# Sums of weight blocks made by accumulating DMA in DRAM instead of on VectorE and GpSimd, and SiLU as a sigmoid with two products

## The chip, the cores and the metric

The kernel runs on one core of a Trainium2 chip. The metric is the time of one execution on the device, in microseconds (us). A core has TensorE (PE in the profile; its weight loads, which overlap its matmuls, are PEld), VectorE (DVE), ScalarE (ACT), GpSimd (POOL) and the queue of SyncE (SP), from which this kernel issues nearly all of its DMAs.

## The reference, cut to what matters

One layer of a streaming encoder: 1024 frames of 1024 features, a token mixer with two branches (HGRN heads and banded attention), a gated feed-forward part, and a gated per-layer input.

```python
h = rmsnorm(x, norm_mix_g[li])
z = h @ w_in[li]
...
merged = (jax.nn.sigmoid(gate_a) * (oa @ w_branch_a[li])
          + jax.nn.sigmoid(gate_b) * (ob @ w_branch_b[li]))
x = x + merged @ w_out[li]
h2 = rmsnorm(x, norm_ffn_g[li])
x = x + (jax.nn.silu(h2 @ w_ffn_gate[li]) * (h2 @ w_ffn_up[li])) @ w_ffn_down[li]
h3 = rmsnorm(x, norm_ple_g[li])
x = x + jax.nn.sigmoid(h3 @ w_ple_gate[li]) * (p[li].astype(x.dtype) @ w_ple_proj[li])
```

`D_FF` is 2816, that is 22 blocks of 128. The change is in how `merged @ w_out`, the feed-forward part's `@ w_ffn_down` and its `silu` are computed.

## The kernel before, in words

Every large product is made from float32 operands that are split in two parts, a rounded high part (`wh`, `whi`: a cast on ACT) and the rest (`wl`, `wlo`: a subtraction, mostly on POOL); TensorE makes three products of these parts. Weights stream from DRAM into raw tiles `wr`, 512 KB each.

The layer runs in stages, one behind the other on TensorE: norm and HGRN heads; attention (from about 290 us to 490); the mixer's gates (500 to 650); branches and output projection (to 820); the feed-forward gate and up projections (820 to 1292); the down projection (1292 to 1550); the per-layer input (to the end).

From the mixer's gates on, the large products use Strassen's scheme in Winograd's form: seven block products in place of eight, of sums of blocks. Of the weights of the output projection (4 groups of four blocks, called quads) and of the down projection (11 quads) the sums are S1 = A21 + A22, S3 = A11 − A21, S2 = S1 − A11 and S4 = A12 − S2. They are made ahead of time and stored in DRAM (`spill`), from where `passes` loads them as weights when the projection comes. A block of a quad is 128 x 512. Sums of the activations (T1 to T4) are made on VectorE, by `branch_sums` for the output projection and by `keep_acts` for the down projection; each product is added into its target by the function that `added` returns.

Who made the weights' sums before: the first five quads (`QUADS = 5`: all four of the output projection and one of the down projection) on POOL in `gate_units`, by `quad_slow`, four POOL additions of 128x512 each; the other ten on VectorE in the feed-forward stage, by `quad_pieces`: two halves per quad, each loaded into one tile named `qd` (its pool has one buffer), four VectorE additions of 128x256, four stores of 128 KB.

The feed-forward stage runs in units, `ff_pairs` looping over units 1 to 21 (unit 0 stands before it). Even units make two blocks of the gate projection, odd ones the same blocks of the up projection. A unit is one call of `strassen`: seven products of 12 matmuls of 512 columns, and VectorE additions of the products in `t` tiles (`u2`, `u3` in the code) and with the row of norm factors `rb`. Between products `strassen` calls `next(side)`: `side` prepares the next unit's weights (`strassen_weights`: block sums `q` on VectorE, casts on ACT, `wlo` on POOL and one on VectorE), the activation sums (`keep_acts`), and pieces of the quads. After each half block, `unit_gate` multiplies by `rb` on VectorE, applies SiLU on ACT and multiplies by `rb` on POOL (the tile `s<-t,rb` on POOL in the profile); `unit_up` multiplies gate and up together.

What sets the order: each engine works strictly in the order in which the program names its instructions (`order` ties each instruction to the one before it on its engine, and so the SP queue too). An instruction that waits holds up all that stand behind it on that engine. Nothing is rescheduled; a `yield` in a generator is the place at which another stream's next step is put. Waits come from data and from tiles whose buffers come free: the feed-forward pools hold 7 `tmp` tiles (`t`) and one `quad` tile (`FFN`).

Most of the profile's lines are the helper's line 54, through which all pinned instructions go; so tiles, not lines, tell them apart.

Of the kernel before, what the change touches and what calls it, by code (L numbers as in the profile page):

```python
# [31 lines left out]
RAW = 2  # L32
AHEAD = 3
PLAIN = 4
QUADS = 5


C_MIX, C_FFN, C_PLE, C_ON, C_GQ, C_GK, C_LB = 0, 8, 16, 24, 25, 26, 27
# [18 lines left out]
class Trunk:  # L57
# [580 lines left out]
    def attention(self):  # L638
# [33 lines left out]
        for i in range(FIRST, 8):  # L672
            next(feed, None)
            if i == FIRST:
                self.hgrn_gate()
            if i == 7:
                drain(stack(0))
                drain(self.hgrn_out())
        for n in range(whole + 2):
            stage(n - 1, 1)  # L680
            next(feed, None)
            if n < whole:
                if steps[n][1] == 0:
# [24 lines left out]
            if n >= whole:  # L708
                next(tail)
            yield 0  # L710
# [83 lines left out]
        while self.kept:  # L794
            self.store(*self.kept.pop(0))

    def gate_units(self, sums):

        V, A = self.V, self.A
        h0, h1 = slice(0, HALF), slice(HALF, T)  # L800
# [39 lines left out]
        for n in range(units):  # L840

            def side():
                more = self.strassen_weights() if n + 1 < units else self.branch_first()
                if n == 0:
                    yield
                    yield
                next(more, None)
                if n + 2 < units:
                    self.strassen_load()
                yield  # L850
                for _ in more:
                    next(sums, None)
                    yield

            self.strassen(lambda c, half, ps: self.gate_done(PLAIN + 2 * n + c, half, ps), side(), early=n == 0)
            yield 0
# [93 lines left out]
    def branch_sums(self, i):  # L950

        m, V = self.m, self.V
        for kind in ("T2", "T1", "T4"):
            m[kind, i] = self.slot()
        V.tensor_tensor(m["B12", i], m["B22", i], m["B12", i], ALU.subtract)
        m["T3", i] = m["B12", i]
        V.tensor_tensor(m["T2", i], m["T3", i], m["B11", i], ALU.add)
        V.tensor_tensor(m["T1", i], m["B22", i], m["T2", i], ALU.subtract)
        V.tensor_tensor(m["T4", i], m["B21", i], m["T2", i], ALU.subtract)


# [49 lines left out]
    def added(self, x):  # L1011

        h0, h1 = slice(0, HALF), slice(HALF, T)
        to = {"A11": ((1, h0), (0, h1), (1, h1)), "S2": ((0, h1),), "A12": ((0, h0),), "S3": ((1, h1),),
              "S1": ((1, h1),), "A22": ((1, h0),), "S4": ((0, h1),)}

        def after(kind, u, ps):
            for odd, h in to[kind]:
                t = x(2 * u + odd)[:, h]
                self.V.tensor_tensor(t, ps, t, ALU.add)  # L1020

        return after

# [21 lines left out]
            if V is self.V:  # L1045
                yield

    def quad_slow(self, jobs):

        G = self.nc.gpsimd  # L1050

        def load(src):
            w = [self.slot() for _ in range(2)]
            for j in range(2):
                self.load(w[j], src[:, j * D:j * D + D])
            return [t[:, i * HALF:i * HALF + HALF] for t in w for i in range(2)]

        def store(parts, k, sums):
            for kind, part in zip(("S2", "S3", "S1", "S4"), parts):
                if k % 2 == 0:  # L1060
                    sums[kind, k // 2] = self.spill()
                self.store(sums[kind, k // 2][:, k % 2 * HALF:k % 2 * HALF + HALF], part)

        cur, prev = load(jobs[0][0]), None
        yield
        yield
        for n, (_, k, sums) in enumerate(jobs):
            a11, a21, a22, a12 = cur
            G.tensor_tensor(a22, a21, a22, ALU.add)
            if prev:  # L1070
                store(*prev)
            yield
            G.tensor_tensor(a21, a11, a21, ALU.subtract)
            yield
            G.tensor_tensor(a11, a22, a11, ALU.subtract)
            prev = cur, k, sums
            if n + 1 < len(jobs):
                cur = load(jobs[n + 1][0])
            yield
            G.tensor_tensor(a12, a12, a11, ALU.subtract)  # L1080
            yield
        store(*prev)

    def quad_pieces(self, jobs):

        V, cols = self.V, HALF // 2
        for src, k, sums in jobs:
            for half in range(2):
                self.n += 1
                w = self.fp.tile([P, 4 * cols], F32, tag="quad", name=f"qd{self.n}")  # L1090
                at = slice(half * cols, half * cols + cols)
                self.load(w[:, :].rearrange("p (i c) -> p i c", i=4), src.rearrange("p (i c) -> p i c", i=4)[:, :, at])
                yield
                yield
                a11, a21, a22, a12 = [w[:, i * cols:i * cols + cols] for i in range(4)]
                V.tensor_tensor(a22, a21, a22, ALU.add)
                V.tensor_tensor(a21, a11, a21, ALU.subtract)
                yield
                V.tensor_tensor(a11, a22, a11, ALU.subtract)
                V.tensor_tensor(a12, a12, a11, ALU.subtract)  # L1100
                yield
                for kind, part in zip(("S2", "S3", "S1", "S4"), (a11, a21, a22, a12)):
                    if k % 2 == 0 and half == 0:
                        sums[kind, k // 2] = self.spill()
                    self.store(sums[kind, k // 2][:, k % 2 * HALF + at.start:k % 2 * HALF + at.stop], part)
                yield

    def quad_plan(self, plain, npairs, sums):
        order = []
# [8 lines left out]


    def out_proj(self):  # L1120
        split, ready = self.m_split, self.m_ready

        def operand(b, i):
# [271 lines left out]
    def unit_gate(self, c, half, ps):  # L1395
# [2 lines left out]
        hs = slice(half * HALF, half * HALF + HALF)  # L1398
        s = self.stmp()
        V.tensor_tensor(g[:, hs], ps, self.rb[:, hs], ALU.mult)  # L1400
        A.activation(s, g[:, hs], AF.Silu)
        G.tensor_tensor(g[:, hs], s, self.rb[:, hs], ALU.mult)

    def unit_up(self, c, half, ps):
        hs = slice(half * HALF, half * HALF + HALF)
# [103 lines left out]
    def keep_acts(self, k):  # L1509
# [5 lines left out]
        def keep(kind, src):  # L1515
# [5 lines left out]
        keep("B21", b[:, h0])  # L1521
        keep("B22", b[:, h1])
        yield
        V.tensor_tensor(a[:, h1], b[:, h1], a[:, h1], ALU.subtract)
        yield
        yield
        V.tensor_tensor(a[:, h0], a[:, h1], a[:, h0], ALU.add)
# [10 lines left out]
    def ff_pairs(self):  # L1538
# [1 line left out]

        units = len(self.sorder)
        self.acts = {}
        pieces = self.quad_pieces(self.later)
        self.strassen_load()
        for n in range(1, units):
            if n % 2 == 0:
# [2 lines left out]
            def side():  # L1549
# [13 lines left out]
                if n % 4 == 0:  # L1563
                    next(pieces, None)
                if n == units - 2:
                    drain(pieces)

            self.strassen((self.unit_gate, self.unit_up)[n % 2], side())
            if n % 2 == 1:
# [3 lines left out]
    def down_plan(self):  # L1573

        n = NFF // 2
        self.aorder = [(b, i, min(D, n * HALF - i * D)) for _, b in self.KINDS for i in range(STEPS)]
        self.plan_weights(self.quad_plan(self.d["dw"], n, self.sums) + self.worder2)
        self.anext, self.araw, self.aready = 0, [], []

# [280 lines left out]
    def run(self):  # L1860
# [18 lines left out]
        with ExitStack() as es:  # L1879
# [24 lines left out]
            with ExitStack() as xs:  # L1904
                self.qp = Small(tc, xs, QUARTERS, "gate_", reuse_waits="tile")
                self.fp = Small(tc, xs, FFN, "gates_", reuse_waits="tile")
                jobs = [(d["oq"][k], k, self.osums) for k in range(4)] + [(d["wq"][k], k, self.sums) for k in range(NFF // 2)]
                drain(self.gate_units(self.quad_slow(jobs[:QUADS])))
                self.later = jobs[QUADS:]
# [158 lines left out]
```

## Time and profile before

| | us |
|---|---|
| median of 3 runs | 1604.16 |
| lowest, highest | 1602.46, 1605.62 |
| the profiled execution | 1605.46 |
| its span in the trace | 1603.7 |
| TensorE busy (share of the span) | 1558.6 (97%) |
| VectorE busy | 1163.0 (73%) |
| GpSimd busy | 652.3 (41%) |
| ScalarE busy | 638.2 (40%) |
| mean granted clock of TensorE | 0.993 |

A profile row of the timeline reads: start, duration, engine, line, operation, output tile <- input tiles, shapes, how many, and in brackets how long the engine had been idle before and what released it. Groups read: line, engine, operation, tiles, count, then busy time and mean duration in ns, then idle time before them and its cause. Buffer numbers are left out of the names: `t` is any temporary, `s` any of the large 128x1024 slots, `pm` a PSUM tile, `d` a spill in DRAM, `q` a block sum of the unit's weights, `in_...` an input of the kernel. "x2" merges two like instructions. The duration of an instruction in the trace holds whatever it waits for once it has been started.

### The profile page before, as it was taken

What the parts mean: (1) busy time and instruction counts of PE and PEld (TensorE: products, weight loads), DVE (VectorE), ACT (ScalarE), POOL (GpSimd) and SP (SyncE); (2) the same over time, 40 slices, a digit from 0 to 9 for tenths busy, and PEclk for the clock granted to TensorE, in tenths of its full rate; (3) what the DMA queues carried; (4) which work ended last, traced back from release to release, by engine and by line L of the source; (5) the groups of instructions that cost most, each with busy time, mean ns of one, the idle gap of its engine ahead of it and who ended that gap; (6) DMA issues with size and microseconds to landing.
All of it is one profiled execution on the core that took longest, in us unless ns stands there. A gap on an engine that the chain in (4) does not pass through costs nothing. (4 is left out here: it accounts for less than half of the span.)

```text
span 1603.7 us, 21710 instructions
## 1 busy us (share of the span) xinstructions
PE 1558.6 (97%) x8224; PEld 1313.0 (82%) x8224; DVE 1163.0 (73%) x1754; ACT 638.2 (40%) x1059; POOL 652.3 (41%) x341
## 2 busy tenths in 40 slices
PE   8999999999999999999999999999999999999997
PEld 6998998888888888888888777777777888888886
DVE  5656656378787787447898898888788867755677
ACT  5221221177676633312566222222222234445462
POOL 3422221313121087335313555544455544644553
PEclk9999999999999999999999999999999999999999
DMA  5101000210202575744445345444444379885334
GB/s 187 53 28 53 27 28 27 99 40 28 86 15 94 190 251 194 289 178 183 132 149 191 124 149 170 151 145 140 141 154 153 123 269 336 297 274 188 125 115 174
DMA packets 95337, 230.40 MB, mean 144 GB/s; under 512 B 9984, under 2 KB 31104, under 8 KB 94720
## 3 DMA queue, kind: packets, MB, share of 16 engines
q1 hardware_dynamic: 95088, 229.00, 41.1%
q8 instruction: 64, 1.05, 0.3%
q14 instruction: 41, 0.34, 0.1%
q10 hardware_dynamic: 144, 0.02, 0.0%
HBM read 163.70 MB, written 65.27 MB: 143 GB/s over the span
## 5 line engine op out<-in xcount | busy, mean ns | idle before, releaser
L83 PE MATMUL pm<-s,wh 128*128 128x512 f32 (+1 forms) x1712 | 531.0, 391 | 6.5 <-ACT wh L123 5.3
L83 PE MATMUL pm<-s,whi 128*128 128x512 f32 x1568 | 489.1, 393 | 20.1 <-DVE t L54 20.1
L126 POOL TENSOR_TENSOR wl<-wr,wh 128x1024 fp32r<-128x1024 f32 (+2 forms) x108 | 267.6, 2483 | 401.1 <-ACT wh L123 397.8
L83 PEld LDWEIGHTS pm<-s,wh 128*128 128x128 f32 x1712 | 319.1, 188 | 73.4 <-ACT wh L123 5.3
L83 PEld LDWEIGHTS pm<-s,whi 128*128 128x128 f32 x1568 | 296.0, 190 | 86.9 <-DVE t L54 25.6
L83 PE MATMUL pm<-s,wl 128*128 128x512 f32 (+1 forms) x856 | 333.3, 389 | 0.5 <-POOL wl L126 0.5
L54 DVE TENSOR_TENSOR s<-s,s 128x512 f32<-128x512 f32 (+4 forms) x217 | 263.5, 1244 | 82.3 <-ACT s L54 44.7
L83 PE MATMUL pm<-s,wlo 128*128 128x512 f32 x784 | 307.3, 392 | 0.0
L83 PE MATMUL pm<-wh,s 128*128 128x256 f32 (+1 forms) x896 | 237.6, 340 | 0.0
L123 ACT CAST wh<-wr 128x1024 fp32r<-128x1024 f32 (+2 forms) x114 | 115.0, 1010 | 270.5 <-PE pm L83 147.6
L83 PEld LDWEIGHTS pm<-s,wl 128*128 128x128 f32 x856 | 160.9, 188 | 34.4 <-POOL wl L126 1.2
L83 PEld LDWEIGHTS pm<-s,wlo 128*128 128x128 f32 x784 | 148.6, 190 | 31.9 <-DVE wlo L54 0.5
L83 PEld LDWEIGHTS pm<-wh,s 128*128 128x128 f32 x896 | 154.4, 190 | 14.0
L54 DVE TENSOR_TENSOR t<-pm,t 128x512 f32<-128x512 f32 x138 | 94.9, 688 | 89.9 <-PE pm L83 83.4
L54 POOL TENSOR_TENSOR wlo<-wr,whi 128x512 fp32r<-128x512 f32 (+1 forms) x53 | 116.2, 2200 | 95.0 <-ACT whi L54 95.0
L54 DVE TENSOR_TENSOR s<-pm,s 128x512 f32<-128x512 f32 (+1 forms) x134 | 87.1, 681 | 89.4 <-PE pm L83 89.2
L83 PE MATMUL pm<-wl,s 128*128 128x256 f32 (+1 forms) x448 | 147.5, 329 | 0.8 <-POOL wl L126 0.8
L54 POOL TENSOR_TENSOR s<-t,rb 128x512 f32<-128x512 f32 x44 | 70.3, 1601 | 115.4 <-ACT t L54 115.4
L54 POOL TENSOR_TENSOR wlo<-q,whi 128x512 fp32r<-128x512 f32 x52 | 83.5, 1606 | 79.5 <-ACT whi L54 73.2
L54 ACT CAST s<-s 128x1024 fp32r<-128x1024 f32 (+1 forms) x94 | 90.0, 980 | 60.7 <-DVE s L54 36.1
L54 ACT CAST whi<-q 128x512 fp32r<-128x512 f32 (+1 forms) x81 | 61.4, 758 | 120.3 <-PE pm L83 98.7
L54 ACT ACTIVATE t<-s 128x512 f32<-128x512 f32 x44 | 27.8, 633 | 167.2 <-DVE s L54 164.3
(145 smaller groups left out, 1856.0 us busy)
## 6 DMA issues: line engine op xcount, KB each, us to landing
s<-d SPq DMA_DIRECT2D x67, 512.0 KB, 5.6
d<-s SPq DMA_DIRECT2D x107, 256.0 KB, 2.6
wr<-d SPq DMA_DIRECT2D x36, 512.0 KB, 3.7
wr<-in_sg SPq DMA_DIRECT2D x22, 512.0 KB, 4.8
wr<-in_su SPq DMA_DIRECT2D x22, 512.0 KB, 4.9
s<-in_x SPq DMA_DIRECT2D x21, 512.0 KB, 7.5
qd<-in_wq SPq DMA_DIRECT2D x20, 512.0 KB, 3.7
d<-qd SPq DMA_DIRECT2D x80, 128.0 KB, 1.9
```

The costliest lines, as they stand in the source:

```text
L54: return lambda *a, **k: self.trunk.order(op(*a, **k), self.key)
L83: return self.order(self.nc.tensor.matmul(*a, **k))
L123: self.nc.scalar.copy(hi[:, c], raw[:, c])
L126: rest.tensor_tensor(lo[:, c], raw[:, c], f32(hi[:, c]), ALU.subtract)
```

## The change

The sums of weights are no longer made by an engine. In the attention loop, `dma_sums` issues one plain copy per step on SP, from the input's block in DRAM to the sum's spill in DRAM (32 copies: 8 of the output projection, 24 of the down projection, each of two quads' blocks, 512 KB). Later, 32 DMAs issued by POOL add a second operand onto the spill in transit (`accum_op=ALU.add`): 8 in `gate_units`, where the POOL additions stood, and 24 in the odd (up) units of `ff_pairs`, up to three per unit. Since such a DMA can only add, the lower blocks' part is taken with the other sign: S3 = A11 + A21, S2 = S1 + A11, S4 = A12 + S2. `added` then subtracts some products in place of adding them, and `branch_sums` and `keep_acts` swap operands. `quad_slow`, `quad_pieces`, the `qd` tile, their loads and stores go.

Two more things: the 128x1024 sum at the end of `keep_acts` is written as two of 128x512; and SiLU in `unit_gate` becomes a Sigmoid on ACT followed by two products on POOL in place of one. The `tmp` pool has 8 tiles in place of 7.

```diff
@@ the attention loop
+        self.osum = self.dma_sums(self.d["oq"], 4, self.osums)
+        self.wsum = self.dma_sums(self.d["wq"], NFF // 2, self.sums)
+        copies = chain(islice(self.osum, 8), islice(self.wsum, 4 * STEPS))
         for n in range(whole + 2):
+            next(copies, None)
             stage(n - 1, 1)
@@ gate_units, side()
-                for _ in more:
-                    next(sums, None)
+                for i, _ in enumerate(more):
+                    if i % 2:
+                        next(self.osum, None)
                     yield
@@ branch_sums
-        V.tensor_tensor(m["B12", i], m["B22", i], m["B12", i], ALU.subtract)
+        V.tensor_tensor(m["B12", i], m["B12", i], m["B22", i], ALU.subtract)
...
@@ added
+        plus, minus = ALU.add, ALU.subtract
+        to = {"A11": ((1, h0, minus), (0, h1, plus), (1, h1, minus)), "S2": ((0, h1, minus),), "A12": ((0, h0, plus),),
+              "S3": ((1, h1, plus),), "S1": ((1, h1, minus),), "A22": ((1, h0, plus),), "S4": ((0, h1, plus),)}
...
-                self.V.tensor_tensor(t, ps, t, ALU.add)
+                self.V.tensor_tensor(t, t, ps, op)
@@ new, in place of quad_slow and quad_pieces
+    def dma_sums(self, src, n, sums):
...
+        for i in jobs:
+            for kind, q in (("S1", 1), ("S3", 0), ("S2", 0), ("S4", 3)):
+                sums[kind, i] = self.spill()
+                self.load(cut(part(kind, i)), block(i, q))
                 yield
...
+        add = lambda out, x: self.G.dma_start(out, x, accum_op=ALU.add, max_dma_last_dim=4 * T)
+        for j in range(0, len(jobs), 2):
+            for kind in ("S1", "S3", "S2", "S4"):
+                for i in jobs[j:j + 2]:
+                    if kind in ("S1", "S3"):
+                        add(cut(part(kind, i)), block(i, 2 if kind == "S1" else 1))
+                    else:
+                        add(part(kind, i), part("S1" if kind == "S2" else "S2", i))
+                    yield
@@ unit_gate
-        A.activation(s, g[:, hs], AF.Silu)
-        G.tensor_tensor(g[:, hs], s, self.rb[:, hs], ALU.mult)
+        A.activation(s, g[:, hs], AF.Sigmoid)
+        G.tensor_tensor(g[:, hs], g[:, hs], s, ALU.mult)
+        G.tensor_tensor(g[:, hs], g[:, hs], self.rb[:, hs], ALU.mult)
@@ keep_acts
-        V.tensor_tensor(
-            b[:, :].rearrange("p (two t) -> p two t", two=2), b[:, :].rearrange("p (two t) -> p two t", two=2),
-            a[:, h0].unsqueeze(1).to_broadcast([P, 2, HALF]), ALU.subtract)
+        V.tensor_tensor(b[:, h0], b[:, h0], a[:, h0], ALU.subtract)
+        V.tensor_tensor(b[:, h1], a[:, h0], b[:, h1], ALU.subtract)
@@ ff_pairs, side()
-                for _ in more:
+                for i, _ in enumerate(more):
                     next(keep, None)
-                    if n > 1:
-                        next(pieces, None)
+                    if n % 2 and i % 2 == 0:
+                        next(self.wsum, None)
                     yield
...
-FFN = {"q1024": 1, "q512": 3, "raw": 2, "tmp": 7, "quad": 1}
+FFN = {"q1024": 1, "q512": 3, "raw": 2, "tmp": 8}
```

On POOL, a gate unit of the feed-forward stage (an `s` written from `t` and `rb` is the last step of `unit_gate`; `wlo` belongs to the next unit's weights) and what follows it in the up unit, before:

```order
L54 TENSOR_TENSOR s_9576<-t_9661,rb_8400 128x512
L54 TENSOR_TENSOR wlo_9642<-wr_9459,whi_9641 128x1024
L54 TENSOR_TENSOR s_9575<-t_9684,rb_8400 128x512
L54 TENSOR_TENSOR wlo_9666<-q_9622,whi_9665 128x512
L54 TENSOR_TENSOR s_9576<-t_9712,rb_8400 128x512
L54 TENSOR_TENSOR s_9575<-t_9737,rb_8400 128x512
L54 TENSOR_TENSOR wlo_9742<-q_9716,whi_9741 128x512
```

And after the change:

```order
L53 TENSOR_TENSOR s_9830<-s_9830,t_9916 128x512
L53 TENSOR_TENSOR s_9830<-s_9830,rb_8393 128x512
L53 TENSOR_TENSOR wlo_9899<-wr_9720,whi_9898 128x1024
L53 TENSOR_TENSOR s_9829<-s_9829,t_9938 128x512
L53 TENSOR_TENSOR s_9829<-s_9829,rb_8393 128x512
L53 TENSOR_TENSOR wlo_9922<-q_9879,whi_9921 128x512
L53 TENSOR_TENSOR s_9830<-s_9830,t_9960 128x512
L53 TENSOR_TENSOR s_9830<-s_9830,rb_8393 128x512
L53 TENSOR_TENSOR s_9829<-s_9829,t_9988 128x512
L53 TENSOR_TENSOR s_9829<-s_9829,rb_8393 128x512
L53 TENSOR_TENSOR wlo_9994<-q_9965,whi_9993 128x512
```

Each of the four half blocks now has two products in a row, and the `wlo` between them stand behind one or more products that were not there.

On POOL, an up unit after the change (before, the same `wlo` stood there without the DMAs; `d` is a spill):

```order
L53 TENSOR_TENSOR wlo_9715<-wr_9559,whi_9714 128x512
L53 DMA d_4377<-d_4216 128x1024
L53 TENSOR_TENSOR wlo_9756<-wr_9561,whi_9755 128x1024
L53 DMA d_4647<-d_4510 128x1024
L53 TENSOR_TENSOR wlo_9775<-q_9736,whi_9774 128x512
L53 DMA d_4436<-d_4377 128x1024
L53 TENSOR_TENSOR wlo_9826<-q_9808,whi_9825 128x512
```

Three DMAs have come in between the `wlo` of the next gate unit.

On VectorE, from the middle of a gate unit on, before (`qd` are the removed sums; `s` from `s` are the activation sums; `t` from `pm` are the additions of products):

```order
L54 TENSOR_TENSOR s_9575<-s_9576,s_9575 128x512
L54 TENSOR_TENSOR qd_9850<-qd_9850 128x256 x2
L54 TENSOR_TENSOR wlo_9940<-q_9906,whi_9939 128x1024
L54 TENSOR_TENSOR qd_9850<-qd_9850 128x256 x2
L54 TENSOR_TENSOR t_9975<-pm_9890,t_9904 128x512
L54 TENSOR_TENSOR t_9975<-pm_9891,t_9975 128x512
L54 TENSOR_TENSOR s_9888<-t_9975,rb_8400 128x512
L54 TENSOR_TENSOR s_9575<-s_9575 128x512
L54 TENSOR_TENSOR s_9887<-pm_9889,rb_8400 128x512
L54 TENSOR_TENSOR s_9576<-s_9576,s_9575 128x1024
```

And after:

```order
L53 TENSOR_TENSOR s_9533<-s_9533,s_9534 128x512
L53 TENSOR_TENSOR wlo_9882<-q_9848,whi_9881 128x1024
L53 TENSOR_TENSOR t_9913<-pm_9832,t_9846 128x512
L53 TENSOR_TENSOR t_9913<-pm_9833,t_9913 128x512
L53 TENSOR_TENSOR s_9830<-t_9913,rb_8393 128x512
L53 TENSOR_TENSOR s_9533<-s_9533 128x512
L53 TENSOR_TENSOR s_9829<-pm_9831,rb_8393 128x512
L53 TENSOR_TENSOR s_9534<-s_9534,s_9533 128x512
L53 TENSOR_TENSOR s_9534<-s_9533,s_9534 128x512
```

The two pairs of `qd` sums around `wlo` are gone, and the one sum of 128x1024 is two of 128x512.

More of the change, by code (lines that the diff above doesn't have):

```diff
@@ L34 @@
 PLAIN = 4
-QUADS = 5
 C_MIX, C_FFN, C_PLE, C_ON, C_GQ, C_GK, C_LB = 0, 8, 16, 24, 25, 26, 27
@@ L795, in gate_keep, with gate_units @@
             self.store(*self.kept.pop(0))
-    def gate_units(self, sums):
+    def gate_units(self):
         V, A = self.V, self.A
@@ L954, in branch_sums @@
             m[kind, i] = self.slot()
-        V.tensor_tensor(m["B12", i], m["B22", i], m["B12", i], ALU.subtract)
+        V.tensor_tensor(m["B12", i], m["B12", i], m["B22", i], ALU.subtract)
         m["T3", i] = m["B12", i]
-        V.tensor_tensor(m["T2", i], m["T3", i], m["B11", i], ALU.add)
-        V.tensor_tensor(m["T1", i], m["B22", i], m["T2", i], ALU.subtract)
+        V.tensor_tensor(m["T2", i], m["B11", i], m["T3", i], ALU.subtract)
+        V.tensor_tensor(m["T1", i], m["T2", i], m["B22", i], ALU.subtract)
         V.tensor_tensor(m["T4", i], m["B21", i], m["T2", i], ALU.subtract)
@@ L1013, in added @@
         h0, h1 = slice(0, HALF), slice(HALF, T)
-        to = {"A11": ((1, h0), (0, h1), (1, h1)), "S2": ((0, h1),), "A12": ((0, h0),), "S3": ((1, h1),),
-              "S1": ((1, h1),), "A22": ((1, h0),), "S4": ((0, h1),)}
+        plus, minus = ALU.add, ALU.subtract
+        to = {"A11": ((1, h0, minus), (0, h1, plus), (1, h1, minus)), "S2": ((0, h1, minus),), "A12": ((0, h0, plus),),
+              "S3": ((1, h1, plus),), "S1": ((1, h1, minus),), "A22": ((1, h0, plus),), "S4": ((0, h1, plus),)}
         def after(kind, u, ps):
-            for odd, h in to[kind]:
+            for odd, h, op in to[kind]:
                 t = x(2 * u + odd)[:, h]
-                self.V.tensor_tensor(t, ps, t, ALU.add)
+                self.V.tensor_tensor(t, t, ps, op)
         return after
@@ L1046, in quad_sums @@
                 yield
[L1048 to L1092, printed above, removed]
-                yield
[L1094 to L1106, printed above, removed]
+    def dma_sums(self, src, n, sums):
+        jobs = range((n + 1) // 2)
+        def block(i, q):
+            m = min(2, n - 2 * i)
+            at = q * HALF
+            return src[2 * i:2 * i + m, :, at:at + HALF].rearrange("k p c -> p k c")
+        def part(kind, i):
+            m = min(2, n - 2 * i)
+            return sums[kind, i][:, :m * HALF]
+        def cut(t):
+            return t.rearrange("p (k c) -> p k c", c=HALF)
+        for i in jobs:
+            for kind, q in (("S1", 1), ("S3", 0), ("S2", 0), ("S4", 3)):
+                sums[kind, i] = self.spill()
+                self.load(cut(part(kind, i)), block(i, q))
+                yield
+        add = lambda out, x: self.G.dma_start(out, x, accum_op=ALU.add, max_dma_last_dim=4 * T)
[7 more added lines that the diff above has]
+                    yield
@@ L1120, in out_proj @@
     def out_proj(self):
+        drain(self.osum)
         split, ready = self.m_split, self.m_ready
@@ L1523, in keep_acts @@
         yield
-        V.tensor_tensor(a[:, h1], b[:, h1], a[:, h1], ALU.subtract)
+        V.tensor_tensor(a[:, h1], a[:, h1], b[:, h1], ALU.subtract)
         yield
         yield
-        V.tensor_tensor(a[:, h0], a[:, h1], a[:, h0], ALU.add)
+        V.tensor_tensor(a[:, h0], a[:, h0], a[:, h1], ALU.subtract)
         yield
-        V.tensor_tensor(
-            b[:, :].rearrange("p (two t) -> p two t", two=2), b[:, :].rearrange("p (two t) -> p two t", two=2),
-            a[:, h0].unsqueeze(1).to_broadcast([P, 2, HALF]), ALU.subtract)
+        V.tensor_tensor(b[:, h0], b[:, h0], a[:, h0], ALU.subtract)
+        V.tensor_tensor(b[:, h1], a[:, h0], b[:, h1], ALU.subtract)
         yield
@@ L1542, in ff_pairs @@
         self.acts = {}
-        pieces = self.quad_pieces(self.later)
         self.strassen_load()
@@ L1556, in side @@
                 yield
-                for _ in more:
+                for i, _ in enumerate(more):
                     next(keep, None)
-                    if n > 1:
-                        next(pieces, None)
+                    if n % 2 and i % 2 == 0:
+                        next(self.wsum, None)
                     yield
                 drain(keep)
[L1563 to L1566, printed above, removed]
             self.strassen((self.unit_gate, self.unit_up)[n % 2], side())
@@ L1576, in down_plan @@
         self.aorder = [(b, i, min(D, n * HALF - i * D)) for _, b in self.KINDS for i in range(STEPS)]
+        drain(self.wsum)
         self.plan_weights(self.quad_plan(self.d["dw"], n, self.sums) + self.worder2)
@@ L1906, in run @@
                 self.fp = Small(tc, xs, FFN, "gates_", reuse_waits="tile")
-                jobs = [(d["oq"][k], k, self.osums) for k in range(4)] + [(d["wq"][k], k, self.sums) for k in range(NFF // 2)]
-                drain(self.gate_units(self.quad_slow(jobs[:QUADS])))
-                self.later = jobs[QUADS:]
+                drain(self.gate_units())
             with ExitStack() as xs:
```

## The prediction

> **What bounds the kernel now.** I read the windows stage by stage first, then TensorE's waits, the chain of waits, and the timelines of VectorE and GpSimd around one stall. A window's row has its bounds and length, then busy time (and instructions) of PE, PEld, DVE, ACT and POOL, the granted clock, the DMA share and GB/s.
>
> ```profile
> 500.00:820.00 320.00, 320.00 (x1492) 265.37 (x1492) 225.59 (x280) 131.54 (x184) 132.04 (x70) 1.00 0.52 184
> 856.00:1291.30 435.30, 414.94 (x1799) 339.05 (x1798) 370.15 (x413) 123.53 (x185) 231.33 (x130) 0.98 0.44 148
> 1292.00:1550.00 258.00, 257.47 (x1151) 213.33 (x1150) 165.79 (x145) 124.11 (x147) 126.90 (x53) 1.00 0.68 240
> 1049.70:1056.50 6.80, 5.98 (x14) 4.72 (x15) 3.20 (x6) 0.00 (x0) 0.00 (x0) 0.50 0.56 200
> 1094.10:1097.50 3.40, 3.27 (x8) 2.59 (x9) 2.06 (x4) 0.00 (x0) 0.00 (x0) 0.50 0.41 145
> 1131.60:1135.00 3.40, 3.40 (x10) 2.64 (x9) 1.62 (x3) 0.56 (x1) 2.77 (x1) 0.50 0.44 154
> ...
> PE pm L83 <- DVE t L54: 20.1, 13, 3.0
> ```
>
> TensorE is the bound. From 500 to 820 (gate units, branches, out projection) and from 1292 to 1550 (down projection) it has no gap worth the name, so work taken off other engines there buys nothing. Only the gate and up units, 856 to 1291, show a loss: 435.30 − 414.94 = 20.4 us idle, of which 20.1 are 13 waits for a VectorE addition into a `t` tile. Three stretches, 13.6 us together, ran at half clock, so 6.8 us more were lost. The prize is 20.1 + 6.8 = 26.9 us.
>
> ```profile
> 883.78 0.73 PE L83 MATMUL pm<-s,whi 128*128 128x512 f32 x2 [3.03 <-DVE t L54]
> 969.63 0.73 PE L83 MATMUL pm<-s,whi 128*128 128x512 f32 x2 [1.67 <-DVE t L54]
> 1009.14 0.73 PE L83 MATMUL pm<-s,whi 128*128 128x512 f32 x2 [1.13 <-DVE t L54]
> 1050.52 1.22 PE L83 MATMUL pm<-s,whi 128*128 128x512 f32 x2 [3.01 <-DVE t L54]
> 1094.23 1.22 PE L83 MATMUL pm<-s,whi 128*128 128x512 f32 x2 [2.52 <-DVE t L54]
> 1130.78 0.73 PE L83 MATMUL pm<-s,whi 128*128 128x512 f32 x2 [2.10 <-DVE t L54]
> ...
> 964.93 1.52 DVE qd L54
> 966.48 2.49 DVE qd L54
> 968.97 0.61 DVE t L54
> 969.63 16.63 PE pm L83 x72
> ```
>
> The first six are single stalls; the chain shows what stands before the second: two pairs of `qd` additions (the sums that the change removes) ahead of the addition into `t`. The chain's 72 matmuls, six products, end at 986.26. Two products later, at 1009.14 − 1.13 = 1008.01, comes the next stall, so eight products take 21.75 us, 2.72 each.
>
> **The change part by part.** *VectorE's sums go.* The 80 additions take 33 us by their median, 73 in fact, because the longest is six times the shortest.
>
> ```profile
> L54 DVE TENSOR_TENSOR qd<-qd x80: 412/426/2610, 908.5 to 1286.0; 128x256 f32<-128x256 f32 x80
> ...
> 990.72 0.68 DVE L54 TENSOR_TENSOR s<-pm,rb 128x512 f32<-128x512 f32 x1
> 991.32 2.82 DVE L54 TENSOR_TENSOR s<-s,s 128x1024 f32<-128x1024 f32 x1
> ...
> 995.76 1.77 DVE L54 TENSOR_TENSOR q<-wr,q 128x512 f32<-128x512 f32 x1
> ...
> 1000.99 0.69 DVE L54 TENSOR_TENSOR t<-pm,t 128x512 f32<-128x512 f32 x1 [0.42 <-ACT t L54]
> ...
> 990.47 2.58 POOL L54 TENSOR_TENSOR wlo<-wr,whi 128x1024 fp32r<-128x1024 f32 x1
> 993.02 2.27 POOL L54 TENSOR_TENSOR s<-t,rb 128x512 f32<-128x512 f32 x1
> 995.25 1.74 POOL L54 TENSOR_TENSOR wlo<-q,whi 128x512 fp32r<-128x512 f32 x1
> 996.95 1.75 POOL L54 TENSOR_TENSOR s<-t,rb 128x512 f32<-128x512 f32 x1
> 999.99 1.75 POOL L54 TENSOR_TENSOR s<-t,rb 128x512 f32<-128x512 f32 x1 [1.29 <-ACT t L54]
> 1001.70 1.74 POOL L54 TENSOR_TENSOR wlo<-q,whi 128x512 fp32r<-128x512 f32 x1
> 1003.39 4.81 POOL L54 TENSOR_TENSOR wlo<-wr,whi 128x512 fp32r<-128x512 f32 x2
> 1008.16 1.45 POOL L54 TENSOR_TENSOR wlo<-q,whi 128x512 fp32r<-128x512 f32 x1
> 1015.42 1.29 POOL L54 TENSOR_TENSOR wlo<-q,whi 128x512 fp32r<-128x512 f32 x1 [5.81 <-ACT whi L54]
> 1018.81 1.29 POOL L54 TENSOR_TENSOR wlo<-wr,whi 128x512 fp32r<-128x512 f32 x1 [2.10 <-ACT whi L54]
> ...
> 1028.67 1.35 POOL L54 TENSOR_TENSOR s<-t,rb 128x512 f32<-128x512 f32 x1 [8.57 <-ACT t L54]
> ```
>
> These two timelines show one change from a gate unit to an up unit that has no `qd` work after 990.7. A VectorE addition with one input in PSUM (`pm`) takes 0.68 whatever POOL does; one with both inputs in SBUF takes 1.77 beside POOL, and POOL's 512 columns take 1.29 alone (1015.42) and 1.75 beside VectorE. The two take turns. The Trainium skill, "SBUF — State Buffer", section "SBUF: two separate sides", says that a GpSimd instruction and a VectorE one that holds both shared read ports do not share, one fully blocks; the 2.82 against 0.68 agrees. By length alone ("VectorE: DVE Perf Modes" gives no more than that) the 33 us would leave and POOL's new multiplications would be free, which makes 1605.5 − 26.9 = 1579; the trace speaks for the lock. In turns, POOL's ops start 1.70 apart (995.25, 996.95); split as 0.68 to 1.29 that is 0.57 for a VectorE op and 1.13 for a POOL op, twice that for 1024 columns.
>
> *GpSimd gets a second multiplication per half gate block, 44 in all*, four in each such transition, and the 128x1024 sum on VectorE becomes two of 512. Done by hand from 990.47 in the new order, the addition for which TensorE waits has ahead of it 7 VectorE ops and POOL's 5 ops of 512 and one of 1024: 7 × 0.57 + 5 × 1.13 + 2.26 + 0.68 = 12.6, so it ends at 1003.1. TensorE needs it six products after 986.26, at 1002.6. Before, it ended at 1001.69, 0.9 ahead. So a stall of 0.5 stands in ten transitions, 5 us. The eleventh (the first, at 883.78) has no `qd` work before either; it keeps its 3.0 and gets one more POOL op ahead, 1.13: 4.2. The late stalls of the up units (969.63, 1009.14) have only `qd` work ahead of them and go; what is late next is the same `t` chain at the transition. The half-clock windows follow the stalls of 3.01, 2.52 and 2.10; none follows those of 1.67 and, at the first transition, 3.03. At 0.5 none is due. Remaining loss 5 + 4.2 = 9.2; gain 26.9 − 9.2 = 17.7. One POOL op more or less ahead in each transition moves this by 1.13 × 10 = 11.
>
> *32 accumulating DMAs are issued by GpSimd*, up to three per up unit in eight up units, eight in the gate units. No GpSimd issue of a large DMA stands in the trace.
>
> ```profile
> s<-d SPq DMA_DIRECT2D x67, 512.0 KB, 5.6
> L78 SPq DMA_DIRECT2D wr<-in_su x22: 327/333/752, 860.4 to 1246.5; - x22
> L556 POOL TENSOR_TENSOR m<-m,mhalf 128x8 f32<-128x8 f32 x16 | 26.2, 1638 | 125.4 <-DVE m L54 125.4
> L477 POOL TENSOR_TENSOR m<-m,mhalf 128x4 f32<-128x4 f32 x8 | 8.1, 1009 | 26.2 <-DVE m L54 25.9
> ```
>
> The issue on SP takes 0.33, the lower bound; a load of 512 KB lands after 5.6, the upper bound if GpSimd were held as long as the data move. GpSimd's own smallest instructions take 1.0 to 1.6; I take 1.5 as the nearest by engine. Room: with four ops more GpSimd ends a transition near 1007.5 (1001.74 + 4 × 1.45); its weight work of the up unit, from 1001.70 on, adds up to 1.74 + 4.81 + 1.45 + 1.29 + 1.29 = 10.6; the next gate op comes at 1028.67. That leaves 1028.67 − 1007.5 − 10.6 = 10.6 us, 3.5 per DMA. At 1.5 they are covered. Queued behind each is a `wlo` of the next gate unit, whose wait for ACT (5.81, 2.10) takes up the delay.
>
> *GpSimd's 20 sums in the gate units go*, and the first reading of the weights moves to the attention.
>
> ```profile
> 324.56 1.16 SPq L78 DMA_DIRECT2D wr<-in_qk  x2
> 376.42 1.06 ACT L123 CAST wh<-wr 128x1024 fp32r<-128x1024 f32 x1
> L54 ACT ACT_TABLE_LOAD x4 | 5.1, 1283 | 2.7 <-DMA d<-t 2.7
> ```
>
> They leave a stage in which TensorE is full: 0. Eight DMAs come, 12 us: 0 as well, since GpSimd works 132 of 320 us there. On SP the 32 copies are issued one per step; the worst place is ten in a row ahead of the attention's weight loads at 324.56, which ACT takes up at 376.42. At 5.6 each, one after the other, ten copies are 56 us against 52 of reserve: between 0 and a few us late; I take 0, because they are moved by many engines at once. Their bytes replace about as many loads and stores, so DMA load in 856 to 1291 falls rather than grows. Two ACT table loads of 1.28 go, beside TensorE: 0. Operand order and signs: 0, the instructions have the same shapes.
>
> Sum: 1605.46 (the profiled execution; 1.3 above the median of 1604.16) − 17.7 = 1587.8. The unclear first transition and 1.5 us of half clock after it make me round up: **1590**.
>
> **Rivals.** *One POOL op more per transition than I counted:* stalls of 1.6 in ten, 5.3 in the first, 21.6 lost against 26.9: 1600. With 0.3 more each, no change, up to 1607. Against it: the order shows where the ops stand, but not how VectorE and POOL fall into turns.
>
> *The lock turns the change over.* If the ops do not overlap at all in turns, the chain takes 7 × 0.68 + 5 × 1.29 + 2.58 + 0.68 = 14.5, ends at 1004.9 and stalls 2.3 us, which is where half clock began (2.1), 3.4 us at 0.5, 1.7 lost. Then 4.0 × 11 = 44, less 26.9: +17, **1623**. It decides from about 2.1 us per transition. For it: the first transition stalls 3.03 with no `qd` work at all, and the change adds POOL work exactly there. Against it: the clean transition at 1001 had 0.9 us in hand.
>
> *GpSimd is held by its DMAs.* At 5.6 each, 3 × (5.6 − 3.5) = 6.3 per up unit, eight times 50: **1639**. It decides from 3.5 + 17.7/24 = 4.2 each. The Trainium skill, "SBUF — State Buffer", same section, warns that GpSimd writes the descriptors itself and that a DMA of 0.62 us took 3.1 beside a VectorE copy; by that, an estimate, three take 9.3, still within the room. No row here shows it.
>
> *The copies come late in the attention:* up to 11 us, 1601. The ten-copy burst speaks for it.
>
> **How the numbers follow.** Main case 0.52 (own range 1579 to 1600: all of the prize, or one POOL op more); one op more 0.06; late copies 0.04; the lock 0.24; DMAs that hold GpSimd 0.14. The range reaches from 1579 up through the lock's 1623 to 1626, and leaves out the DMA case. A measurement can tell about 0.2% (3.2 us) from no change. Faster: the main case nearly whole and half of the late copies, 0.54; same 0.08; slower 0.38.
>
> **What would show it.** Right: TensorE's waits for `DVE t` fall from 20 us to about 10, all at the change from gate to up unit, none late in the up units; no stretch at 0.5; the windows 500 to 820 and 1292 to 1550 unchanged in length. The lock shows as eleven waits of 2 to 4 us and stretches at 0.5 behind them; the DMAs as GpSimd late with `wlo` and TensorE waiting for `wlo`; late copies as ACT's cast waiting for `wr` near 376. I would be wrong if the transition's chain has more in it than the seven VectorE ops.

## The result, and the profile after

The changed kernel takes 1599.78 us (median of 6 runs, 1598.88 to 1601.13) where the kernel before, beside it, takes 1605.46: a ratio of 0.9966, 95% interval 0.9953 to 0.9979. That is 0.34% faster, 5.7 us; from 1605.46 the forecast of 1590 is 15.5. The direction held and so did the range, but the size is little more than a third.

The windows of the changed kernel, in the prediction's columns; the last row is the gate and up units from their first matmul to the last addition:

```profile
500.00:820.00 320.00, 320.00 (x1495) 265.48 (x1494) 219.15 (x282) 132.29 (x184) 104.40 (x58) 1.00 0.51 165
856.00:1291.30 435.30, 419.87 (x1828) 342.29 (x1828) 386.97 (x346) 126.49 (x188) 320.06 (x198) 0.99 0.48 131
1292.00:1550.00 258.00, 257.44 (x1152) 213.40 (x1151) 167.27 (x149) 124.92 (x149) 127.73 (x54) 1.00 0.66 233
857.61:1285.70 428.09, 412.92 (x1790) 336.39 (x1791) 384.10 (x341) 123.80 (x184) 314.54 (x195) 0.99 0.49 132
```

The same stretch of the kernel before was 856.87 to 1291.20:

```profile
856.87:1291.20 434.33, 414.23 (x1792) 338.42 (x1792) 369.78 (x411) 122.66 (x183) 231.23 (x130) 0.98 0.44 148
```

So the stage is 6.2 us shorter, which covers the whole gain: the spans of the two profiled executions, 1603.7 and 1598.8, differ by 4.9, so the rest of the program takes 1.3 longer. The two other stages in the table are as full as they were. GpSimd is busy for 314.5 us of it in place of 231.2, and VectorE, from which 80 sums have been taken, is busy longer than before.

What TensorE waits for in that stage now (us in total, times, longest), and six of the single waits:

```profile
PE pm L82 <- DVE t L53: 14.4, 14, 4.6
PE pm L82 <- POOL wlo L53: 0.7, 2, 0.6
...
883.63 0.74 PE L82 MATMUL pm<-s,whi 128*128 128x512 f32 x2 [1.28 <-DVE t L53]
925.00 1.22 PE L82 MATMUL pm<-s,whi 128*128 128x512 f32 x2 [2.50 <-DVE t L53]
946.68 0.73 PE L82 MATMUL pm<-s,whi 128*128 128x512 f32 x2 [0.95 <-DVE t L53]
966.43 0.73 PE L82 MATMUL pm<-s,whi 128*128 128x512 f32 x2 [0.41 <-DVE t L53]
1048.98 1.22 PE L82 MATMUL pm<-s,whi 128*128 128x512 f32 x2 [4.63 <-DVE t L53]
1150.43 0.74 PE L82 MATMUL pm<-s,whi 128*128 128x512 f32 x2 [1.19 <-DVE t L53]
...
924.90:928.80 3.90, 3.80 (x11) 3.07 (x12) 3.35 (x3) 1.47 (x2) 3.82 (x3) 0.61 0.00 0
1049.00:1054.00 5.00, 5.00 (x12) 3.94 (x13) 3.23 (x2) 1.35 (x2) 4.92 (x4) 0.50 0.00 0
```

The wait of 0.41 is the rule at the change from gate to up unit; 2.50 and 4.63 are two exceptions, and behind each stands a window at a low clock: 3.9 × 0.39 + 5.0 × 0.50 = 4.0 us lost. Waits and clock make 14.4 + 0.7 + 4.0 = 19.1, where the prediction left 9.2.

The two exceptions stand behind GpSimd's DMAs. GpSimd's timeline of the first up unit, and later DMAs with and without a wait, in the changed kernel:

```profile
892.31 1.10 POOL L53 DMA_DIRECT2D d<-in_wq  x1
...
899.75 1.08 POOL L53 DMA_DIRECT2D d<-in_wq  x1 [3.90 <-issue]
...
909.34 1.06 POOL L53 DMA_DIRECT2D d<-in_wq  x1 [7.18 <-PE pm L82]
909.94 1.78 POOL L53 TENSOR_TENSOR wlo<-q,whi 128x512 fp32r<-128x512 f32 x1
911.19 1.77 POOL L53 TENSOR_TENSOR wlo<-wr,whi 128x512 fp32r<-128x512 f32 x1
912.43 1.77 POOL L53 TENSOR_TENSOR s<-s,t 128x512 f32<-128x512 f32 x1
914.28 1.63 POOL L53 TENSOR_TENSOR s<-s,rb 128x512 f32<-128x512 f32 x1
...
933.67 1.08 POOL L53 DMA_DIRECT2D d<-in_wq  x1
...
936.62 1.38 POOL L53 DMA_DIRECT2D d<-d  x1
...
942.10 0.81 POOL L53 DMA_DIRECT2D d<-d  x1 [2.78 <-issue]
...
1137.22 1.06 POOL L53 DMA_DIRECT2D d<-in_wq  x1
1140.18 1.32 POOL L53 DMA_DIRECT2D d<-in_wq  x1
...
d<-in_wq POOLq DMA_DIRECT2D x10, 512.0 KB, 7.7
...
909.69 5.07 DVE L53 TENSOR_TENSOR s<-s,s 128x512 f32<-128x512 f32 x1
1030.13 5.22 DVE L53 TENSOR_TENSOR s<-s 128x512 f32<-128x512 f32 x1
```

The DMA itself takes 0.8 to 1.4 us of GpSimd. But the second one from `in_wq` starts 7.44 us after the first, and the third 9.6 after that. By the profile's record of the DMAs the first needed 7.1 us to land and the second 9.2 (the median is 7.7), so each held one started 0.3 to 0.4 after the one ahead had landed. The profile finds no releaser that explains it ("issue", or a TensorE product long done). A `d<-d` behind one from `in_wq` is issued at once (936.62), a third DMA waits again (942.10). The rows fit a limit on what is in flight: a DMA from `in_wq` has 256 rows of 2 KB, one from `d` has 128 of 4 KB; 256 + 128 passes, 256 + 256 and 256 + 128 + 128 do not until the first has landed. The source does not explain it: the DMA at 1140.18 comes from `in_wq` too, but it serves the last, single quad with 128 rows, and it goes out without a wait behind one of 256 rows. Then, with GpSimd late, its waiting work runs without a gap (909.94, 911.19, 912.43: 1.25 apart, its pace alone), and the VectorE addition in between lasts 5.07.

### The profile page after: what moved, and what is told of

Same layout as the page of the kernel before. It is cut to its first block, busy times and chain, and to the rows that moved or that the text cites. A ratio compares the mean times of both kernels' runs of the same rounds, so it can differ in the third digit from the quotient of the medians.

```text
span 1598.8 us, 21535 instructions
## 1 busy us (share of the span) xinstructions
PE 1559.1 (98%) x8224; PEld 1312.8 (82%) x8224; DVE 1171.8 (73%) x1685; ACT 636.9 (40%) x1057; POOL 712.5 (45%) x397
## 4 chain that ended last, share of the span: by engine, by line
PE 75%; DVE 15%; issue 3%; ACT 1%; DMA 1%; POOL 1%; SPq 0%; DVEq 0%; POOLq 0%; ACTq 0%
PE pm L82 72%; DVE s L53 8%; DVE q L53 3%; PE pm L85 3%; DVE t L53 2%; DVE m L53 1%; DMA d<-s 1%; DVE pm L53 0%; ACT s L53 0%; POOL wl L125 0%; DMA wr<-in_fm 0%; ACT wh L122 0%; POOL m L555 0%; ACT m L53 0%; DVE wlo L53 0%
## 5 line engine op out<-in xcount | busy, mean ns | idle before, releaser
L82 PE MATMUL pm<-s,whi 128*128 128x512 f32 x1568 | 487.8, 392 | 14.4 <-DVE t L53 14.4
L53 DVE TENSOR_TENSOR s<-s,s 128x512 f32<-128x512 f32 (+3 forms) x228 | 273.2, 1230 | 79.2 <-ACT s L53 41.7
L53 POOL TENSOR_TENSOR s<-s,t 128x512 f32<-128x512 f32 x44 | 73.1, 1662 | 66.6 <-ACT t L53 66.6
L82 PEld LDWEIGHTS pm<-wl,s 128*128 128x128 f32 x448 | 85.4, 191 | 5.9 <-POOL wl L125 0.6
```

Source lines behind the costliest of these rows:

```text
L53: return lambda *a, **k: self.trunk.order(op(*a, **k), self.key)
L82: return self.order(self.nc.tensor.matmul(*a, **k))
```

## The experiments

Two theories to begin with. R: the rows in flight hold GpSimd back, and the large stalls come from that. L: the second product on GpSimd alone makes the transitions late, as in the prediction's rival of the lock. All ratios are against the kernel before, run beside them; its median was 1605.52 in the first four and 1603.50 in the last three.

**SiLU back, DMA sums kept.**

```diff
-        A.activation(s, g[:, hs], AF.Sigmoid)
-        G.tensor_tensor(g[:, hs], g[:, hs], s, ALU.mult)
-        G.tensor_tensor(g[:, hs], g[:, hs], self.rb[:, hs], ALU.mult)
+        A.activation(s, g[:, hs], AF.Silu)
+        G.tensor_tensor(g[:, hs], s, self.rb[:, hs], ALU.mult)
```

> The changed kernel with SiLU as before (ACT Silu, one GpSimd product per half block); the DMA sums stay. Theory R (outstanding rows of the accumulating DMAs hold GpSimd: with 384 rows in flight the next DMA is issued at once, with 512 it waits until the first has landed, GpSimd's queue backs up, VectorE is locked out some 5 us, and the stalls of 2.50 and 4.63 us with the half clock behind them come from that): the waits of 3.9 to 7.2 us before GpSimd's DMAs stay, the two large stalls shrink by at most 2.3 each (two products fewer ahead) but do not go; the small stalls of 0.41 to 0.57 at the transitions go. 4 to 8 us faster than the changed kernel: 1592 to 1596. Theory L (the second product on GpSimd alone makes the transitions late): all stalls go, half clock too, about 1582.

Measured: 1580.77 us (1579.70 to 1583.29), ratio 0.9854 (0.9829 to 0.9878). R missed by 11 us or more, L was within 1.3. But the trace shows that what R says of GpSimd is there all the same:

```profile
PE pm L82 <- DVE t L53: 2.4, 2, 2.1
...
895.04 1.08 POOL L53 DMA_DIRECT2D d<-in_wq  x1 [4.49 <-issue]
...
904.41 1.06 POOL L53 DMA_DIRECT2D d<-in_wq  x1 [6.98 <-issue]
...
906.26 1.77 POOL L53 TENSOR_TENSOR wlo<-wr,whi 128x512 fp32r<-128x512 f32 x1
909.34 1.30 POOL L53 TENSOR_TENSOR s<-t,rb 128x512 f32<-128x512 f32 x1 [1.30 <-ACT t L53]
...
1041.14 5.17 DVE L53 TENSOR_TENSOR s<-t,s 128x512 f32<-128x512 f32 x1
```

The DMAs wait as long as before, a VectorE addition of 512 columns is still locked out for 5.17 us, and TensorE does not notice: by 909.34 GpSimd has caught up and waits for ACT again. So neither theory alone. It takes both, held DMAs and two products.

**The same DMAs with 128 rows.**

```diff
-                        add(cut(part(kind, i)), block(i, 2 if kind == "S1" else 1))
+                        add(part(kind, i), part("S4", i))
```

> The changed kernel, but the accumulating DMAs of S1 and S3 add the spill of S4 in place of the input's block: the same number, place, bytes and order of DMAs, but 128 rows of 4 KB in place of 256 of 2 KB (the sums S1 and S3 are thereby not those of the reference). Theory R: no more than 384 rows are in flight, the waits of 3.9 to 7.2 us before the DMAs go or fall under 2, the stalls 2.50 and 4.63 fall to about 0.45, no half clock: 2.05 + 4.18 + 4.0 = 10 us faster than the changed kernel, about 1589.5. Theory L: as the changed kernel, 1599.8.

Measured: 1588.61 us (1587.38 to 1589.57), ratio 0.9900 (0.9881 to 0.9919), R's 1589.5. The second product is still there; the waits behind DMAs of 256 rows have gone:

```profile
892.14 0.90 POOL L53 DMA_DIRECT2D d<-d  x1
895.12 1.13 POOL L53 DMA_DIRECT2D d<-d  x1
896.92 1.40 POOL L53 DMA_DIRECT2D d<-d  x1
...
1057.14 0.83 POOL L53 DMA_DIRECT2D d<-d  x1 [3.47 <-issue]
...
923.88 0.73 PE L82 MATMUL pm<-s,whi 128*128 128x512 f32 x2 [0.41 <-DVE t L53]
...
PE pm L82 <- DVE t L53: 6.3, 11, 1.3
...
L53 DVE TENSOR_TENSOR s<-t,s x33: 691/1592/5370, 888.2 to 1288.8; 128x512 f32<-128x512 f32 x33
```

Three DMAs of 128 rows go out within 4.8 us of each other, and the transition at 924, which stalled 2.50, stalls 0.41. One wait of 3.47 us is left, where R allowed 2 at most. It is of another kind: this DMA (an S4) adds the sum S2 that the DMA two ahead of it is still making, and it starts soon after that one has landed; the changed kernel has the same wait at 1062.12 (2.20, released by `DMA d<-d`). With the same products, bytes and count, 11.2 us depend on how many rows a DMA has, or on its source, which this edit changes with the rows; the DMA at 1140.18 above speaks for the rows.

**No accumulating DMAs in the up units.**

```diff
-                    if n % 2 and i % 2 == 0:
-                        next(self.wsum, None)
...
-        drain(self.wsum)
```

> The changed kernel without the 24 accumulating DMAs of the down projection's sums (so these sums stay copies of one block); the copies, the signs and the sigmoid stay. Theory R: the two large stalls and those of 0.95 and 1.19 behind the other late DMAs go, the stalls of about 0.42 stay: 1587 to 1589. Theory L: 1598 or more.

Measured: 1585.83 us (1584.90 to 1586.70), ratio 0.9883 (0.9863 to 0.9902), 1.2 better than R's lower end. What is left are the stalls of 0.41 (and 1.29 at the first transition): 5.0 in 10 waits. The VectorE additions `s<-t,s` that had lasted up to 4.5 us in the changed kernel, and 5.4 with 128 rows, now end by 2.4, and the longest VectorE addition of 512 columns in the stage is one of 2.89:

```profile
PE pm L82 <- DVE t L53: 5.0, 10, 1.3
...
922.15 0.73 PE L82 MATMUL pm<-s,whi 128*128 128x512 f32 x2 [0.41 <-DVE t L53]
...
L53 DVE TENSOR_TENSOR s<-t,s x33: 692/1001/2362, 888.1 to 1285.6; 128x512 f32<-128x512 f32 x33
...
878.12 2.89 DVE L53 TENSOR_TENSOR q<-wr,wr 128x512 f32<-128x512 f32 x1
```

So the lock-outs of 4 to 5 us come with the DMA itself, waits or not; with two products and hardly a wait left the DMAs cost 1588.61 − 1585.83 = 2.8 us.

**Two DMAs per up unit, 384 rows at most.** The order of the 24 is written out, four of them go behind the eight in the mixer's gate units, and each up unit issues two, one of 128 rows and one of 256 or 128.

```diff
+PACED = [("S1", 0), ("S1", 1), ("S3", 0), ("S3", 1)] + [
+    ("S" + c, int(i)) for c, i in "20 12 21 13 40 32 41 33 22 14 23 34 42 15 43 35 24 25 44 45".split()]
...
+        early = chain(self.osum, islice(self.wsum, 4))
...
-                    if n % 2 and i % 2 == 0:
+                    if n % 2 and i in (0, 2):
                         next(self.wsum, None)
```

> The changed kernel with the same 32 accumulating DMAs in another order and place: four of the down projection's in the last gate units of the mixer, the other 20 two per up unit, one of them with 256 rows at most, so that no more than 384 rows are in flight. Theory R: as without the DMAs but for their own second of issue: no wait over 1 us before a DMA, no stall over 1.3, no half clock, 1588 to 1591. Theory L: 1599.8, since GpSimd's products and the count of DMAs are the same.

Measured: 1593.66 us (1592.26 to 1598.19), ratio 0.9935 (0.9912 to 0.9958). In the up units R holds for the waits, as no DMA waits over a microsecond, and nearly for the stalls: one of 1.51 passes its limit of 1.3. But the whole is 2.7 us over R's upper end, since the stage begins later, at 860.69 in place of 857.61. The last of the four early DMAs is held, too, and keeps a weight of the branches (`wl`) waiting behind it; a little later TensorE has four gaps of 1.4 us together that the changed kernel does not have. The other 1.7 us of the delay I cannot place.

```profile
656.71 1.07 POOL L55 DMA_DIRECT2D d<-in_wq  x1 [2.17 <-issue]
657.31 5.25 POOL L127 TENSOR_TENSOR wl<-wr,wh 128x1024 fp32r<-128x1024 f32 x2
...
669.34 0.51 PE L84 MATMUL pm<-s,wh 128*128 128x512 f32 x1 [0.76 <-DVE s L194]
...
860.69 0.50 PE L84 MATMUL pm<-ph,wh 128*128 128x512 f32 x1 [0.26 <-DVE m L216]
```

After these four the theory was S: the second product and the held DMAs draw on the same spare time of GpSimd at the transition, and only what exceeds it costs. Three more runs put that to the test.

**The gate of the change alone, on the kernel before:** the first experiment's diff the other way round, on the kernel before.

> The kernel before, with only the gate of the change: Sigmoid on ACT and two GpSimd products per half block; the sums of weights stay on VectorE and GpSimd. Theory S (slack: the second product costs little where GpSimd has time to spare at the transition, and much where something else has used it up): here VectorE's qd sums have used it up, each of the 11 transitions gets two GpSimd operations more ahead, 1.4 to 2.3 us each, 15 to 25 in all, and half clock where a stall passes 2.1: 1620 to 1640. Rival: the product costs the same wherever it stands, about 4 to 6 us as the eleven stalls of 0.41 show without DMAs: 1610 to 1612.

Measured: 1631.22 us (1630.13 to 1635.14), ratio 1.0175 (1.0154 to 1.0195): slower by 28 us, within S's range and far outside the rival's. TensorE's stalls reach 4.9:

```profile
PE pm L83 <- DVE t L54: 36.1, 15, 4.9
```

So the second product costs more where the transition has less to spare. Whose time is short is not shown by this run: no DMA stands on GpSimd in these up units, and what fills the transition here are VectorE's sums.

**SiLU and no accumulating DMAs in the up units:** the first and the third diff together.

> The changed kernel with SiLU and one product, and without the 24 accumulating DMAs of the down projection's sums (these sums stay copies of one block). Theory S: with one product GpSimd has the time for the DMAs and for the lock-outs of VectorE behind them, so leaving them out buys nothing: 1579 to 1581, the same as with them (1580.8). Rival: each DMA costs by itself (its second of issue, its 4 us lock-out of VectorE): 5 us or more faster, 1576 or less.

Measured: 1579.66 us (1578.58 to 1584.02), ratio 0.9855 (0.9835 to 0.9876), against 0.9854 with the DMAs. With one product the 24 DMAs, their waits and their lock-outs cost nothing that can be told.

**The split of the 128x1024 sum alone, on the kernel before.**

```diff
-        V.tensor_tensor(
-            b[:, :].rearrange("p (two t) -> p two t", two=2), b[:, :].rearrange("p (two t) -> p two t", two=2),
-            a[:, h0].unsqueeze(1).to_broadcast([P, 2, HALF]), ALU.subtract)
+        V.tensor_tensor(b[:, h0], b[:, h0], a[:, h0], ALU.subtract)
+        V.tensor_tensor(b[:, h1], b[:, h1], a[:, h0], ALU.subtract)
```

> The kernel before, with only the sum of 128x1024 at the end of the activation sums written as two of 128x512. Theory S: the work is the same, 1604 to 1607. Rival: two short operations get into turns with GpSimd where one long one waited once, so VectorE loses a turn (about 1.2 us) at each of ten transitions: 1612 or more; or gains as much.

Measured: 1606.30 us (1604.06 to 1612.50), ratio 1.0019 (1.0006 to 1.0033): 1 to 5 us slower. The median lies in S's range, the rival's 8 or more is excluded. In its profiled execution (1610.22, above the median) TensorE's 13 waits for `t` come to 23.3 us, against 20.1 in as many waits before; why they are longer stays open.

Put together, in us (medians):

| sums of the down projection | SiLU, one product | Sigmoid, two products | the second product costs |
|---|---|---|---|
| on VectorE (kernel before) | 1605.5, 1603.5 | 1631.2 | 26 to 28 |
| by DMA as in the change | 1580.8 | 1599.8 | 19 |
| by DMA, 128 rows each | not run | 1588.6 | |
| left out | 1579.7 | 1585.8 | 6 |

The medians stand beside two different ones of the kernel before; by the ratios to it the last column reads 28, 18 and 4.5.

The 24 DMAs cost 1 us beside one product and 14 beside two. The change is thus two changes of opposite sign: everything but the gate is worth 1.5%, and the second product takes most of it back. The 1.5% holds the sums by DMA, the split sum and the eighth `tmp` tile together; the split was slower by itself, the eighth tile was not run by itself. The version with SiLU, 1580.77, beats both kernels.

## Why the prediction was right or wrong

**The prize.** Right. 26.9 us were to be had in the gate and up units, 1579 at best; SiLU with DMA sums reaches 1580.8, and the stages put down as worth nothing gave nothing.

**The VectorE sums.** Right: with them went the late stalls of the up units; without DMAs there is none, and the four of 0.4 to 1.2 in the changed kernel stand behind held DMAs. The chain of seven VectorE and five and a half GpSimd operations also held: the forecast stall of 0.5 at a transition is 0.41, in the changed kernel as without DMAs. At the first transition 4.2 were forecast and 1.28 came: it starts from the end of the stage before it, not from a steady state, and differed from kernel to kernel (2.12 with SiLU, 1.29 without DMAs, 0.60 with the gate alone). What sets it is not shown, and I had no ground to carry its 3.0 over.

**The DMAs on GpSimd: the step that failed.** "The issue on SP takes 0.33, the lower bound; a load of 512 KB lands after 5.6, the upper bound [...] I take 1.5 [...] At 1.5 they are covered." Their instruction takes 0.8 to 1.4, as taken, but a second price was missing: the wait before it, up to 7.2 us, until an earlier DMA has landed. The rival "GpSimd is held by its DMAs" had named the mechanism with a wrong price: it would have taken 50 us and come to 1639, because I counted each of three DMAs as held for its landing, and because I let all that exceeds the room reach TensorE. In fact two units of eight, those with three DMAs of 256 rows, were held for 11.1 us (3.90 + 7.18) and 10.7 (4.44 + 6.29), more than the whole room of 10.6, so that GpSimd was late for its gate products, and those cost: (2.50 − 0.41) + (4.63 − 0.41) = 6.3 us of stalls and 4.0 of half clock, with 3.2 more in waits of 0.4 to 1.2 within four up units, each behind a third DMA that had waited 1.7 to 2.8; the first transition gave 2.9 back. The prediction's "At 1.5 they are covered" thus put at nothing a term that measured about 11. The run with 128 rows puts all of the holding at 11.2 us.

**The second product.** Its cost was sized as if it stood alone: 5 + 1.1 us, and it is 4.5 to 6 where no DMA stands before it. What the sum did not have is that two terms drew on one reserve. The room of 10.6 us per up unit was charged with the DMAs, the transition with the products, each by itself covered or nearly so; GpSimd's waits tell how the reserve went. Before, in 856 to 1292:

```profile
POOL s L54 <- ACT t L54: 115.4, 24, 8.6
POOL wlo L54 <- ACT whi L54: 87.7, 23, 10.5
```

After:

```profile
POOL s L53 <- ACT t L53: 66.6, 10, 8.6
...
POOL d L53 <- issue: 22.0, 6, 6.3
POOL wlo L53 <- ACT whi L53: 10.0, 8, 3.6
POOL d L53 <- PE pm L82: 8.9, 2, 7.2
POOL d L53 <- DMA d<-d: 2.7, 2, 2.2
```

203 us of waiting for ACT became 77, and of 24 waits for the gate's activation 10 are left. The second products took part of this time, the held DMAs the rest; the last line is the wait for a sum that another DMA is still making.

**The lock.** The Trainium skill, "SBUF — State Buffer", section "SBUF: two separate sides", has one port pair that the two engines share and that is locked for a whole instruction; a VectorE instruction with two SBUF inputs takes it against a GpSimd one that reads SBUF. The trace agrees where no GpSimd DMA is near: turns, about 1.7 us apart. The prediction's rival gave the whole change stalls over 2.1 with half clock behind them, 1623. The gate alone did this to the kernel before: 1631, with eight stalls of 2.1 to 4.9 and a low clock behind six of them. With the same gate and VectorE's sums gone, the run without DMAs has ten stalls, 5.0 in all, so the room came with the rest of the change, of which the removed sums are the largest part. The same section of the Trainium skill warns that a DMA issued by GpSimd is slowed when VectorE holds the shared ports in a two-port operation such as a copy. Here, beside VectorE's additions, the trace shows the other direction: the DMA's instruction kept its 0.8 to 1.4 us, and VectorE waited.

**The rest.** The copies did not come late: the attention's stage, 290 to 500, has TensorE busy for 206.48 of 210 us (206.54 before), and ACT's wait for `wr` from `in_qk` is 1.0 us in place of 2.0; nothing on record gives the 11 us that this rival was priced at. The split sum, taken at about nothing, cost 1 to 5 us on the kernel before. The sum's terms do not close entirely: waits and clock fell by 26.9 − 19.1 = 7.8, the stage by 6.2; the 1.6 between them I cannot place. Three slips in the working change nothing: the 80 additions come to 34 us by their median, not 33; the turn of 1.70 splits into 0.59 and 1.11, which leaves the chain at 12.6; and 50 us on 1587.8 give 1638.

## What to carry to other kernels

When a change both takes work off an engine and puts other work on a neighbour, charge all of it against one account of that neighbour's spare time, at the place where its result is waited for; two additions that are each covered may not be covered together. A queue's price is not only its instruction: look for what limits how much may be in flight, and keep DMAs with many short rows apart. And run the halves of a two-part change by themselves: here one was worth −1.5% and the other cost +1.2% on top.

## What the runs showed of the hardware that was not expected

DMAs issued by GpSimd stop being issued when too many rows are in flight. In all runs here 384 rows in flight were let through (256 + 128, or three of 128), and what would have made 512 waited until the first DMA had landed, whether it was 256 + 256, 256 + 128 + 128 or 128 + 128 + 256, and in the stage of the mixer's gates as in the up units. In the changed kernel the held DMA started 0.2 to 0.4 us after that landing, which came 7.0 to 9.3 us after the first one's issue. Bytes do not decide: three DMAs of 512 KB pass with 128 rows each, and one of 256 KB with 128 rows is held behind 384 rows (at 1104.84, for 1.68 us). The exact limit, and whether rows or the descriptors made of them count, was not tried.

Behind a GpSimd DMA the turns between GpSimd and VectorE fail for two or three operations: GpSimd's additions follow one another 1.25 us apart, its pace alone, and a VectorE addition of 512 columns with two inputs in SBUF lasts up to 5.6 us, where in the runs without such DMAs the longest lasts 2.9. This stands behind DMAs of 256 rows and of 128. What causes it is open.
